# Settling three quarters of an FFN's output with factor and residual ahead of their last product

## The chip, the cores and the metric

The kernel runs on one core of a Trainium2 chip. The metric is device time in microseconds (us). The engines of the core run side by side, each through its own list of instructions in order: PE (matrix products), DVE (VectorE, elementwise), ACT (ScalarE, elementwise and functions), POOL (hardly used here), and SP, whose queue issues nearly all DMA transfers. PE writes to eight PSUM banks of 128x512 values; DVE and ACT read them.

## The reference, cut to what matters

One layer on 1024 tokens of width 1024, in float32: an FFN, a mixing sub-layer, a second FFN, a final norm. Each FFN adds half of its output to what came in:

```python
def rmsnorm(x, g):
    y = xf * lax.rsqrt(jnp.mean(xf * xf, axis=-1, keepdims=True) + NORM_EPS)
    return y * g

def swiglu_ffn(x, w_in, w_out):
    gate, up = jnp.split(x @ w_in, 2, axis=-1)
    return (jax.nn.silu(gate) * up) @ w_out
...
h = h + 0.5 * swiglu_ffn(rmsnorm(h, norm_ffn1), ffn1_w_in, ffn1_w_out)
u = rmsnorm(h, norm_mix)
proj = u @ w_in            # q, k, v, gates, pool: the mixing sub-layer follows
...
h = h + 0.5 * swiglu_ffn(rmsnorm(h, norm_ffn2), ffn2_w_in, ffn2_w_out)
return rmsnorm(h, norm_final)
```

The norm's root is one number per token. The kernel leaves it out of the products and multiplies the results by it afterwards; `rb` below is that row of numbers, halved (the 0.5), spread over the 128 partitions.

## The kernel before

Activations lie transposed: eight tiles `mt` of 128 channels by 1024 tokens. A *quarter* is one of these tiles on one half `j` of the tokens, 128x512. Products are made from pairs of float32r values, a high and a low part (`split`: ACT copies the high part, L158, DVE subtracts for the low part, L159), so each 128x128 by 128x512 product is three matmuls (`mm3`, L178 to L180).

All large products use Strassen's scheme in Winograd's form: seven block products in place of eight, whose sums make the four blocks of the result. The change is in `ffn_out`, the second half of an FFN. It is called twice: "b" after the first FFN, followed by the projections of the mixing sub-layer, and "d" after the second, followed by the end of the kernel (`last` is set there). Names in profile rows begin with that letter: `bacc` is a quarter or tile of b's result, `bp2w` the weight of step p2 in b, `bp2m` its moving operand, `bres` a residual, `brb` the factor row, `bL` the weight halves `L12` and `L22`, `br`, `bq`, `bT` and `bR` loaded activations.

`ffn_out` runs its block products in this order, each as FH = 11 steps over `k`, and each step on four banks `i`, that is twelve matmuls: p1 and p6 interleaved, p2 and p7 interleaved, p5, p3, and in b p4. In d p4 is made the other way round, tokens on the partitions: four tiles of 128 tokens, two in the steps `near`, two in `far`, which end the kernel. Banks "a" hold p1, then p1+p2; then p5, then p5+p3. Banks "b" hold p6, then p6+p7, then (in b) p4 too. After the last `k` of a product, `after1` to `after7` read each bank as soon as it is done:

- after p1: a copy of the bank to `p1s` (ACT). After p6: quarter (i, 1) = bank + `p1s` (`onto`).
- after p2: quarter (i, 0) = bank x `rb`, and `done`: plus the residual.
- after p7: quarter (i+4, 1) = bank + `p1s`. In b `p1s` is copied by ACT to quarter (i+4, 0); in d that quarter is bank + `p1s` and then `done`.
- after p5: quarter (i+4, 1) += bank, `done`. After p3: quarter (i, 1) += bank, `done`. After p4 (b): quarter (i+4, 0) += bank, `done`.

`done` puts a function `end` into a list of background work: scale the quarter by `rb` (L933; left out after p2), add the residual `old` (L941), hand the quarter to the next stage (`mix.quarter` in b: store it, square it on ACT, L264, and sum the squares, L265). With these four tiles finished, `end1` puts the next norm's operands into the list: R11 after p2, R22 after p5, T2, T1, T3 after p3, R21 and T4 after p4 (`n2R`, `n2T`), and at the end the norm's sums and root (`n2sum`, `n2v`, `n20b`, `n21b`). `t0` and `t1` are the first two groups of projections: `t0wL`, `t0wS` are weights, `t0a`, `t0b`, `t0e` banks, `t0v` a copy of a bank.

What sets the order: each step is a pair of functions. `Flow.run` calls the first (`prep`: loads, splits) four steps ahead of the second (`body`: the matmuls), and after each body takes two pieces of background work. A planner then orders the instructions on each engine; those within `soon()` have a high priority. Buffers come from small pools: `raw` has four tiles of 128x1024 (weight halves and residuals), `tl` four, `c2` eight of 128x512, `wt` five weights. A load is issued on SP's queue, in order, when the buffer that it fills is free. `residual(mts, j, tile, two)` loads the residuals of four quarters into two tiles of the pool named (or four of `c2`); it is called at k = FH - 3 of p2, p5, p3 and p4 (b) or p7 (d).

Of the kernel before, what the change touches and what calls it, by code (L numbers as in the profile page):

```python
# [15 lines left out]
ADD, SUB, MUL = ALU.add, ALU.subtract, ALU.mult  # L16
# [8 lines left out]
FH = FT // 2  # L25
# [65 lines left out]
def block_kernel(ctx: ExitStack, tc, x, x_tok, vecs, f1_in, f1_out, w_in, w_v, pool_w, w_ret, w_pool, w_o,  # L91
# [3 lines left out]
    tt = nc.vector.tensor_tensor  # L95
    stt = nc.vector.scalar_tensor_tensor
    act = nc.scalar.activation
    copy = nc.scalar.copy
    soon = tc.high_priority
    flow = Flow()  # L100
# [16 lines left out]
    def raw(name):  # L117
        return sb.tile([P, S], F32, tag="raw", bufs=N_RAW, name=name)

    def tl(name):  # L120
        return sb.tile([P, S], F32, tag="tl", bufs=N_TL, name=name)
# [4 lines left out]
    def c2(name):  # L126
        return sb.tile([P, H], F32, tag="c2", bufs=N_C2, name=name)
# [4 lines left out]
    def sum_bank(name):  # L132

        return ps.tile([P, H], F32, tag="sum", bufs=N_SUM, name=name)

    def load(dst, src):
        nc.sync.dma_start(dst, src)
# [8 lines left out]
    def half(t, j):  # L146
        return t[:, j * H : (j + 1) * H]
# [49 lines left out]
    for n in range(N_SUM):  # L197
        b = sum_bank(f"set{n}")
# [614 lines left out]
    def ffn_out(nx, ops, ready, w, res, name, sink, end, last=None):  # L813
# [4 lines left out]
        t, acc, old, p1s = {}, {}, {}, {}  # L818
# [4 lines left out]
            t["rb"] = sb.tile([P, S], F32, tag="mv", bufs=N_MV, name=f"{name}rb")  # L823
            act(t["rb"], nx.rms(), AF.Copy, scale=0.5)

        def residual(mts, j, tile, two=2):
            for n in range(0, 4, two):
                r = tile(f"{name}res{mts[n]}{j}")
                for z, mt in enumerate(mts[n : n + two]):
                    load(half(r, z), res[mt][:, j * H : (j + 1) * H])  # L830
                    old[mt, j] = half(r, z)

        TOP, LOW = range(4), range(4, 8)
# [6 lines left out]
        def both(key, k, src):  # L840

            if k % 2 == 0:
                t[key] = (tl if key[0] != "L" else raw)(f"{name}{key}{k}")
                n = min(2, FH - k)
                for z in range(n):
                    load(half(t[key], z), src(k + z))
            return half(t[key], k % 2)
# [21 lines left out]
            return s2, half(t["r"], 1)  # L869

        def p2(k):
            if k == FH - 3:
                residual(TOP, 0, raw)
            r = tl(f"{name}q{k}")
            load(half(r, 0), T[k][:, :H])
            load(half(r, 1), B[k][:, H:])
            t["r"] = r
            L12, s2 = both("L12", k, lambda z: w[z, :, 3 * H :]), half(S2[k // 2], k % 2)

            tt(s2, L12, s2, SUB)  # L880
            return L12, half(r, 0)

        def p7(k):
            if last and k == FH - 3:
                residual(LOW, 0, c2, 1)
            return half(S3[k // 2], k % 2), half(t["r"], 1)

        def p5(k):
            if k == FH - 3:
                residual(LOW, 1, raw)  # L890
            return half(S1[k // 2], k % 2), both("T1", k, lambda z: B[z][:, :H])

        def p3(k):
            if k == FH - 3:
                residual(TOP, 1, raw)
            return half(S2[k // 2], k % 2), both("R22", k, lambda z: T[z][:, H:])

        def p4(k):
            if not last and k == FH - 3:
                residual(LOW, 0, tl)  # L900
            return both("L22", k, lambda z: w[z, :, 2 * H : 3 * H]), both("T4", k, lambda z: T4[z])

        bk = {}
# [20 lines left out]
        def quarter(mt, j):  # L924
            return half(acc[mt], j)

        def onto(mt, j, where, i, before=None):
            q = quarter(mt, j)
            with soon():
                tt(q, bk[where, i], q if before is None else before, ADD)  # L930

        def scale(q, src, j):
            tt(q, src, half(t["rb"], j), MUL)  # L933

        def done(mt, j, to=sink, scaled=False):
            q = quarter(mt, j)

            def end():
                if not scaled:
                    scale(q, q, j)  # L940
                tt(q, q, old.pop((mt, j)), ADD)  # L941
                if to:
                    to(mt, slice(j * H, (j + 1) * H), acc[mt])

            flow.add(end)
# [4 lines left out]
                copy(p1s[i], bk["a", i])  # L950

        def after6(i):
            onto(i, 1, "b", i, p1s[i])

        def after2(i):
            with soon():
                scale(quarter(i, 0), bk["a", i], 0)
            done(i, 0, scaled=True)
            if i == 3:
                end(2)  # L960

        def after7(i):
            onto(i + 4, 1, "b", i, p1s[i])
            if last:

                onto(i + 4, 0, "b", i, p1s[i])
                done(i + 4, 0, None)
                if i == 3:
                    flow.add(*last.turned(acc))
            else:  # L970
                copy(quarter(i + 4, 0), p1s[i])

        def after5(i):
            onto(i + 4, 1, "a", i)
            done(i + 4, 1)
            if i == 3:
                end(5)

        def after3(i):
            onto(i, 1, "a", i)  # L980
            done(i, 1)
            if i == 3:
                end(3)

        def after4(i):
            onto(i + 4, 0, "b", i)
            done(i + 4, 0)
            if i == 3:
                end(4)

        for k in range(FH):
            yield step("p1", p1, k, "a", True, after1)
            yield step("p6", p6, k, "b", True, after6)
        for k in range(FH):
            yield step("p2", p2, k, "a", False, after2)
            yield step("p7", p7, k, "b", False, after7)
        for k in range(FH):
            yield step("p5", p5, k, "a", True, after5)
        for k in range(FH):
            yield step("p3", p3, k, "a", False, after3)  # L1000
        if not last:
            for k in range(FH):
                yield step("p4", p4, k, "b", False, after4)
            return
# [6 lines left out]
        def near(k):  # L1011
            def prep():
                l, r = p4(k)
                scale(r, r, 0)
                L[k], X[k] = operand(l, f"{name}p4w{k}"), mv(f"{name}p4m{k}")
                split(X[k][:, 0], X[k][:, 1], r)

            def body():
                if k == 1:

                    last.seed(2, bk["a", 0])
                    last.seed(3, bk["a", 1])
                for n in range(2):
                    turned(n, k)
                    if k == FH - 1:
                        last.finish(n)

            return prep, body
# [692 lines left out]
    class Last(Norm):  # L1721
# [76 lines left out]
        def end(self, part):  # L1798
            if part != 3:
                return  # L1800
            tokens = slice(H, S)
            at = {}

            def stats():
                r = inverse_root(token_sums(self.ssq, range(tokens.start // P, tokens.stop // P), "fin0"), D, "fin0")
                at["b"] = spread(r, "fin0")

            def scale(mt):
                t = self.tiles[mt][:, tokens]
                stt(t, t, vec[:, V_FINAL + mt : V_FINAL + mt + 1], at["b"], MUL, MUL)  # L1810
                load(out[mt, :, tokens], t)

            flow.add(stats, *(lambda mt=mt: scale(mt) for mt in range(KT)))
# [97 lines left out]
```

## Time and profile before

| what | value |
| --- | --- |
| time, median of 3 runs | 2169.99 us (2167.82 to 2172.97) |
| the profiled execution | 2169.06 us |
| its span, first to last instruction | 2167.2 us |
| mean granted TensorE clock | 0.996 |
| PE matmul, busy | 2145.4 us, 99% |
| DVE, busy | 1837.3 us, 85% |
| ACT, busy | 1091.1 us, 50% |
| DMA traffic | 320.91 MB, mean 148 GB/s |
| b: first p1 matmul to first p5 matmul | 423.5 to 543.2 us |

Rows of a profile are read so: in a table by stretch, the stretch in us, its length, then busy time (and count) of PE, PEld (weight loads, which overlap PE), DVE, ACT and POOL, the granted TensorE clock, the share of the DMA engines, and GB/s. In a timeline: start, duration, engine, line, operation, output<-inputs by the program's names, sizes, how many were merged into the row, and in brackets how long the engine had been idle and what ended the wait. DVE and ACT instructions overlap a little at their ends, so the distance of starts is what one costs. Matmuls too: each row has 0.39 us, while one starts every 0.23.

### The profile page before, as it was taken

How to read it: one execution, taken by the hardware profiler on the slowest of the kernel's cores; microseconds unless marked ns; L12 is line 12 of the kernel's file. 1: busy time of each engine (PE TensorE's matmuls, PEld its weight loads, DVE VectorE, ACT ScalarE, POOL GpSimd, SP SyncE). 2: the span in 40 equal slices, each digit the busy share in tenths (PEclk: the TensorE clock that was granted, in tenths of full speed). 3: DMA queues.
4: the chain of work that ended last, by engine and by line, in shares of the span. 5: the costliest groups of instructions: out<-in, count | busy, mean ns of one | idle time of the engine just before them, and what ended most of it. 6: DMA issues, size and time to landing. Idle time of an engine off the chain costs nothing.

```text
span 2167.2 us, 29645 instructions
## 1 busy us (share of the span) xinstructions
PE 2145.4 (99%) x10668; PEld 1815.0 (84%) x10668; DVE 1837.3 (85%) x3223; ACT 1091.1 (50%) x2053; POOL 0.2 (0%) x4
## 2 busy tenths in 40 slices
PE   9999999999989999999999999999999999999998
PEld 7888888888877888888888998887888888888887
DVE  8788888995897798899867877899988888889597
ACT  8544444553645444444435754446644544445454
POOL 0000000000000000000000000000000000000000
PEclk9999999999998999999999999999999999999999
DMA  7232423584532333233485567624223232358543
GB/s 260 87 114 82 136 75 128 182 287 137 184 128 102 117 113 121 88 127 108 160 276 181 166 206 255 246 91 159 74 85 135 74 127 93 127 176 287 184 122 126
DMA packets 120131, 320.91 MB, mean 148 GB/s; under 512 B 13232, under 2 KB 17456, under 8 KB 119984
## 3 DMA queue, kind: packets, MB, share of 16 engines
q1 hardware_dynamic: 119408, 317.98, 43.6%
q8 instruction: 83, 1.36, 0.3%
q10 hardware_dynamic: 576, 1.05, 0.1%
q14 instruction: 64, 0.52, 0.1%
HBM read 228.27 MB, written 90.70 MB: 147 GB/s over the span
## 4 chain that ended last, share of the span: by engine, by line
PE 91%; DVE 6%; ACT 1%; DMA 1%; issue 1%; SPq 0%; ACTq 0%; DVEq 0%
PE c_b L178 2%; PE c_b L180 2%; PE c_b L179 2%; PE a_b L178 2%; PE a_b L180 2%; PE a_b L179 2%; PE c_e L178 2%; PE c_e L179 2%; PE c_e L180 2%; PE a_e L178 2%; PE a_e L179 2%; PE a_e L180 2%; PE c_a L179 1%; PE a_a L178 1%; PE c_a L178 1%; PE c_a L180 1%
## 5 line engine op out<-in xcount | busy, mean ns | idle before, releaser
L179 PE MATMUL c_b<-n3T,c_wS 128*128 128x512 f32 x176 | 68.5, 389 | 0.0
L180 PE MATMUL c_b<-n3T,c_wS 128*128 128x512 f32 x176 | 68.5, 389 | 0.0
L178 PE MATMUL c_b<-n3T,c_wS 128*128 128x512 f32 x176 | 68.2, 389 | 0.0
L179 PE MATMUL a_b<-n1T,a_wS 128*128 128x512 f32 x168 | 65.4, 389 | 0.0
L178 PE MATMUL a_b<-n1T,a_wS 128*128 128x512 f32 x168 | 65.4, 389 | 0.0
L180 PE MATMUL a_b<-n1T,a_wS 128*128 128x512 f32 x168 | 65.4, 389 | 0.0
L179 PE MATMUL a_a<-n1R,a_wL 128*128 128x512 f32 x120 | 46.7, 389 | 0.0
L178 PE MATMUL a_a<-n1R,a_wL 128*128 128x512 f32 x120 | 46.7, 389 | 0.0
L180 PE MATMUL a_a<-n1R,a_wL 128*128 128x512 f32 x120 | 46.7, 389 | 0.0
L179 PE MATMUL c_a<-n3R,c_wL 128*128 128x512 f32 x112 | 43.7, 390 | 0.0
L178 PE MATMUL c_a<-n3R,c_wL 128*128 128x512 f32 x112 | 43.6, 389 | 0.0
L180 PE MATMUL c_a<-n3R,c_wL 128*128 128x512 f32 x112 | 43.6, 389 | 0.0
L178 PEld LDWEIGHTS c_b<-n3T,c_wS 128*128 128x128 f32 x176 | 33.0, 188 | 6.9
L180 PEld LDWEIGHTS c_b<-n3T,c_wS 128*128 128x128 f32 x176 | 33.0, 188 | 6.9
L179 PEld LDWEIGHTS c_b<-n3T,c_wS 128*128 128x128 f32 x176 | 33.0, 188 | 6.8
L159 DVE TENSOR_TENSOR a_wS<-a_S,a_wS 128x512 fp32r<-128x512 f32 x45 | 30.6, 682 | 9.1 <-ACT a_wS L158 9.0
L180 PEld LDWEIGHTS a_b<-n1T,a_wS 128*128 128x128 f32 x168 | 31.5, 188 | 6.6
L179 PEld LDWEIGHTS a_b<-n1T,a_wS 128*128 128x128 f32 x168 | 31.5, 188 | 6.5
L178 PEld LDWEIGHTS a_b<-n1T,a_wS 128*128 128x128 f32 x168 | 31.5, 188 | 6.5
L159 DVE TENSOR_TENSOR c_wS<-c_S,c_wS 128x512 fp32r<-128x512 f32 x46 | 31.3, 681 | 3.6 <-ACT c_wS L158 3.6
L178 PE MATMUL c_e<-n3T,c_wS 128*128 128x512 f32 x88 | 34.4, 391 | 0.0
L178 PE MATMUL c_e<-n3T,c_wL 128*128 128x512 f32 x88 | 34.4, 391 | 0.0
(3061 smaller groups left out, 8045.2 us busy)
## 6 DMA issues: line engine op xcount, KB each, us to landing
c_ra<-in_f_in SPq DMA_DIRECT2D x22, 512.0 KB, 3.5
c_rb<-in_f_in SPq DMA_DIRECT2D x22, 512.0 KB, 4.1
a_ra<-in_f_in SPq DMA_DIRECT2D x21, 512.0 KB, 3.7
a_rb<-in_f_in SPq DMA_DIRECT2D x21, 512.0 KB, 4.3
t<-au SPq DMA_DIRECT2D x11, 512.0 KB, 4.2
b<-ag SPq DMA_DIRECT2D x11, 512.0 KB, 3.6
r<-au SPq DMA_DIRECT2D x11, 512.0 KB, 3.6
br<-r SPq DMA_DIRECT2D x11, 512.0 KB, 5.3
```

Source lines behind the costliest of these rows:

```text
L159: tt(lo, src, hi.bitcast(F32), SUB)
L178: mm(dst, w[0], m[0], start=start, stop=False, skip_group_check=True)
L179: mm(dst, w[0], m[1], start=False, stop=False, skip_group_check=True)
L180: mm(dst, w[1], m[0], start=False, stop=stop, skip_group_check=True)
```

## The change

Three of the four groups of quarters that wait for a second product are *settled* while that product runs: the sum so far is multiplied by `rb` and the residual is added (`settle`). When the last product's bank is ready, it is multiplied by `rb` on its way out of PSUM into a `c2` tile `d`, and `d` is added to the quarter (`done`). So by linearity (sum + bank) x rb + residual becomes (sum x rb + residual) + bank x rb.

- Quarters (i, 1) are settled from k = 4 of p2 on, quarters (i+4, 0) from k = 8 of p2 on, straight out of `p1s` (so that ACT's copies in b go), quarters (i+4, 1) from k = 5 of p5 on.
- Quarters (i, 0) are not settled; their residual is added together with `d` after p2.
- The residuals are loaded in p2 at k = 1, 5 and 9 and in p5 at k = 1, all into `raw` tiles.

```diff
-        def residual(mts, j, tile, two=2):
-            for n in range(0, 4, two):
-                r = tile(f"{name}res{mts[n]}{j}")
-                for z, mt in enumerate(mts[n : n + two]):
+        def residual(mts, j):
+            for n in (0, 2):
+                r = raw(f"{name}res{mts[n]}{j}")
+                for z, mt in enumerate(mts[n : n + 2]):
                     load(half(r, z), res[mt][:, j * H : (j + 1) * H])
                     old[mt, j] = half(r, z)
...
         def p2(k):
-            if k == FH - 3:
-                residual(TOP, 0, raw)
+            if k == 1:
+                residual(TOP, 1)
+            if k == 4:
+                flow.add(*(lambda i=i: settle(i, 1) for i in range(4)))
+            if k == 5:
+                residual(LOW, 0)
+            if k == 8:
+                flow.add(*(lambda i=i: settle(i + 4, 0, p1s[i]) for i in range(4)))
+            if k == 9:
+                residual(TOP, 0)
...
         def p7(k):
-            if last and k == FH - 3:
-                residual(LOW, 0, c2, 1)
...
         def p5(k):
-            if k == FH - 3:
-                residual(LOW, 1, raw)
+            if k == 1:
+                residual(LOW, 1)
+            if k == 5:
+                flow.add(*(lambda i=i: settle(i + 4, 1) for i in range(4)))
...
         def p3(k):
-            if k == FH - 3:
-                residual(TOP, 1, raw)
...
         def p4(k):
-            if not last and k == FH - 3:
-                residual(LOW, 0, tl)
...
-        def onto(mt, j, where, i, before=None):
-            q = quarter(mt, j)
+        def onto(mt, j, where, i):
             with soon():
-                tt(q, bk[where, i], q if before is None else before, ADD)
+                tt(quarter(mt, j), bk[where, i], p1s[i], ADD)
...
-        def done(mt, j, to=sink, scaled=False):
+        def settle(mt, j, src=None):
+
             q = quarter(mt, j)
+            scale(q, q if src is None else src, j)
+            tt(q, q, old.pop((mt, j)), ADD)
+
+        def done(mt, j, where, i, to=sink):
+            q, d = quarter(mt, j), c2(f"{name}d{mt}{j}")
+            with soon():
+                scale(d, bk[where, i], j)
 
             def end():
-                if not scaled:
-                    scale(q, q, j)
-                tt(q, q, old.pop((mt, j)), ADD)
+                tt(q, old.pop((mt, j), q), d, ADD)
...
         def after2(i):
-            with soon():
-                scale(quarter(i, 0), bk["a", i], 0)
-            done(i, 0, scaled=True)
+            done(i, 0, "a", i)
...
         def after7(i):
-            onto(i + 4, 1, "b", i, p1s[i])
+            onto(i + 4, 1, "b", i)
             if last:
-                onto(i + 4, 0, "b", i, p1s[i])
-                done(i + 4, 0, None)
+                done(i + 4, 0, "b", i, None)
                 if i == 3:
                     flow.add(*last.turned(acc))
-            else:
-                copy(quarter(i + 4, 0), p1s[i])
...
         def after5(i):
-            onto(i + 4, 1, "a", i)
-            done(i + 4, 1)
+            done(i + 4, 1, "a", i)
```

`after3` and `after4` change as `after5` does. Nothing else in the kernel changes; in the changed kernel the bank reads by `rb` and the scalings of a settling are on L936, `onto` on L933, the residual of a settling on L942, the last add on L950, and the line L880 has become L888.

More of the change, by code (lines that the diff above doesn't have):

```diff
@@ L952, in after6 @@
         def after6(i):
-            onto(i, 1, "b", i, p1s[i])
+            onto(i, 1, "b", i)
         def after2(i):
-            with soon():
-                scale(quarter(i, 0), bk["a", i], 0)
-            done(i, 0, scaled=True)
+            done(i, 0, "a", i)
             if i == 3:
@@ L979, in after3 @@
         def after3(i):
-            onto(i, 1, "a", i)
-            done(i, 1)
+            done(i, 1, "a", i)
             if i == 3:
@@ L985, in after4 @@
         def after4(i):
-            onto(i + 4, 0, "b", i)
-            done(i + 4, 0)
+            done(i + 4, 0, "b", i)
             if i == 3:
```

## The prediction

> **What bounds the kernel now.** I read the page first, then the busy time by stretches, then the two stretches in which PE is not full, instruction by instruction on PE, DVE and ACT.
>
> ```profile
> PE 2145.4 (99%) x10668; PEld 1815.0 (84%) x10668; DVE 1837.3 (85%) x3223; ACT 1091.1 (50%) x2053; POOL 0.2 (0%) x4
> PE 91%; DVE 6%; ACT 1%; DMA 1%; issue 1%; SPq 0%; ACTq 0%; DVEq 0%
> 600.00:700.00 100.00, 90.58 (x379) 72.93 (x378) 87.64 (x161) 54.55 (x98) 0.00 (x0) 0.93 0.31 103
> 2130.00:2140.00 10.00, 9.11 (x45) 7.43 (x44) 9.39 (x17) 4.13 (x6) 0.00 (x0) 1.00 0.01 2
> ```
>
> PE bounds the whole: 99% busy, 91% of the chain. The second half of an FFN, `ffn_out`, runs from 423 to 633 us ("b") and again at the end ("d"). In it PE is full but for 0.89 us in the last row (DVE 9.39 of 10). Between 600 and 700, where b hands over to the projections, PE loses 9.42 us and part of its clock (0.93). So two places can give time back, and a stall anywhere else in b or d costs. PE at the handover:
>
> ```profile
> 633.37 0.39 PE L178 MATMUL t0a<-n2R,t0wL 128*128 128x512 f32 x1
> 633.60 0.39 PE L179 MATMUL t0a<-n2R,t0wL 128*128 128x512 f32 x1
> 636.94 0.50 PE L180 MATMUL t0a<-n2R,t0wL 128*128 128x512 f32 x1 [2.50 <-DVE t0wL L159]
> 650.38 0.80 PE L178 MATMUL t0b<-n2T,t0wS 128*128 128x512 f32 x1 [3.18 <-ACT t0v L479]
> 654.39 0.63 PE L178 MATMUL t0b<-n2T,t0wS 128*128 128x512 f32 x1
> 654.82 0.63 PE L179 MATMUL t0b<-n2T,t0wS 128*128 128x512 f32 x1
> 658.57 1.84 PE L228 MATMUL n2sum<-cst,n2ssq 128*128 128x1 f32 x16
> 668.19 0.78 PE L246 MATMUL n20b<-n20dg,ones_r 128*128 128x512 f32 x2 [2.17 <-ACT n20dg L245]
> 670.53 1.22 PE L246 MATMUL n21b<-n21dg,ones_r 128*128 128x512 f32 x2 [1.57 <-ACT n21dg L245]
> ```
>
> Four waits: 2.50 for a weight's low part, 3.18 for the copy `t0v`, 2.17 and 1.57 for the norm's factor. Starts lie 0.23 us apart at full clock (633.37, 633.60) and 0.43 after the second wait: 12 matmuls of half clock, 12 x 0.20 = 2.4 us more. DVE and ACT behind them:
>
> ```profile
> 601.79 2.48 DVE L930 TENSOR_TENSOR bacc<-bp5a,bacc 128x512 f32<-128x512 f32 x4
> 604.19 1.28 DVE L933 TENSOR_TENSOR bacc<-bacc,brb 128x512 f32<-128x512 f32 x2
> 605.39 1.29 DVE L941 TENSOR_TENSOR bacc<-bacc,bres 128x512 f32<-128x512 f32 x2
> 632.61 2.47 DVE L930 TENSOR_TENSOR bacc<-bp6b,bacc 128x512 f32<-128x512 f32 x4
> 636.21 0.68 DVE L159 TENSOR_TENSOR t0wL<-t0ra,t0wL 128x512 fp32r<-128x512 f32 x1
> 648.51 0.68 DVE L941 TENSOR_TENSOR bacc<-bacc,bres 128x512 f32<-128x512 f32 x1
> 661.03 0.15 DVE L214 TENSOR_SCALAR n2v<-n2sum 128x8 f32<-128x8 f32 x1
> 663.42 0.16 DVE L221 SCALAR_TENSOR_TENSOR n2r<-n2t,n2r 128x8 f32<-128x8 f32 x1
> 649.23 0.63 ACT L264 ACTIVATE n2q<-bacc 128x512 f32<-128x512 f32 x1 [1.16 <-DVE bacc L941]
> 666.63 0.19 ACT L158 CAST n20r<-n2r 128x4 fp32r<-128x4 f32 x1
> ```
>
> DVE works through one list without a rest. Both kernels can be built without running them, which gives the order of instructions on each engine (called the list here) and no times. In the list of before, 56 instructions stand from the first bank read of p3's end (601.79) to `t0wL` (636.21): 34.42/56 = 0.615 each, and 0.60 for a plain one, reading a bank or not (four from 601.79 to 604.19, two from there to 605.39). The last residual add (648.51) frees the fourth square on ACT (649.23), and only behind that comes `t0v`. The handover is bound by DVE's list.
>
> **The change, part by part.** Removed: at p5's, p3's and p4's ends a quarter took twelve DVE instructions (four bank reads, four scalings, four adds); now eight (four scaled bank reads into `d`, four adds). Where p2 ends the count stays eight. Also gone: b's four ACT copies at p7's end. Added: three settlings of eight DVE instructions in each of b and d, two in p2/p7 and one in p5. Per `ffn_out` DVE goes from 52 to 64 here, for both +24 x 0.60 = 14.4 us. What matters is the place.
>
> *b's handover.* From p3's end on the list loses the eight scalings, and small weight steps change places with the bank reads of p4's end, which the built order puts later.
> - `t0wL` is the 47th of the list, not the 57th: 601.79 + 46 x 0.615 = 630.1. PE wants it after 633.8, so the 2.50 goes, with 3 us to spare. p4's own operands, first needed by PE at 603, come no later than before.
> - The bank reads now come at 601.79 + 56 x 0.615 = 636.2 to 638.6. PE reaches `t0b` in those banks at 633.37 + 24 x 0.227 = 638.8, and the copies into them fit between on ACT. Cost nothing; if DVE is 2 us late there, PE waits that long.
> - The last add is the 68th, not the 77th: 648.51 - 9 x 0.60 = 643.1. From its start to PE's restart took 650.38 - 648.51 = 1.87, so `t0v` is ready at 645.0. PE is through the 48 matmuls ahead of it at 633.37 + 48 x 0.227 = 644.3. A wait of 0.7 stays of 3.18, and with so short a gap I take the half clock to go: 24 matmuls at 0.227 = 5.4, `n2sum` at 650.4 in place of 658.57, 8.2 earlier.
> - Late next is the root of the norm. `n2v` is the 89th, not the 97th: 661.03 - 8 x 0.60 = 656.2; root ready 2.55 later (661.03 to 663.58) at 658.8. The cast `n20r` (666.63) follows a cast that waits for PE, now at 658.4; so it runs at 658.9, 7.7 earlier. From there all keeps its distances. **b gives 7.7.** Bounds: 2.5, if only the first wait goes, and 10.1, if a second half clock goes too.
>
> *d's end.* The chain there:
>
> ```profile
> 2097.29 2.47 DVE L930 TENSOR_TENSOR dacc<-dp5a,dacc 128x512 f32<-128x512 f32 x4
> 2098.18 0.40 PE L178 MATMUL dp5a<-dp3m,dp3w 128*128 128x512 f32 x1
> 2138.94 1.02 PE L228 MATMUL fin0sum<-cst,n4ssq 128*128 128x1 f32 x8 [0.89 <-DVE n4ssq L265]
> ```
>
> The sum of squares comes four scalings (2.4) sooner, but the built order also puts `fin0sum` 11 matmuls (2.5) sooner: the 0.89 stays. At p5's end a bank must be read before p3 reuses it; 0.3 us were to spare (2097.29 + 0.60 against 2098.18), and the list ahead has one instruction fewer or more by how ACT and the loads fall. Bounds: 0.9 gained to 1.0 lost; taken 0, the count being level.
>
> *p2/p7: new work and moved loads.* Sixteen more DVE instructions, 9.6 us:
>
> ```profile
> 490.00:540.00 50.00, 50.00 (x222) 41.43 (x221) 24.94 (x40) 19.46 (x34) 0.00 (x0) 1.00 0.44 138
> 483.37 0.39 PE L178 MATMUL bp1a<-bp2m,bp2w 128*128 128x512 f32 x1
> 527.75 0.69 DVE L159 TENSOR_TENSOR bp2w<-bL,bp2w 128x512 fp32r<-128x512 f32 x1 [2.03 <-ACT bp2w L158]
> bL<-in_f_out SPq DMA_DIRECT2D x3, 256.0 KB, 3.8
> DMA to landing us min/median/max: 3.3/5.1/6.3
> ```
>
> DVE has 25 of 50 us free, so the instructions are covered. The loads are the risk. The residual tiles now sit in two of the four `raw` buffers, so an `L12` pair can be asked for only when the last split of the pair before is done; on SP's queue it stands behind residual loads that wait for a settling, and the operand loads behind it wait with it. DVE's list stops at the subtraction (L880, now L888) until the pair lands, 3.8 us by the group of these loads. I followed three pairs through the built lists: DVE stands up to 2 us at each, and the lead of 483.37 + 10 x 5.44 - 528.4 = 9.4 us that a `p2` weight has over PE (5.44 is (543.2 - 483.37)/11, a step of p2 and one of p7) falls to about 5.6. Cost nothing; without that cover, whatever a landing is longer than 3.8 + 5.6/3 = 5.7 us, three times a stage. The residual loads are the same bytes as before, only sooner. POOL's queue and ACT's have no part in it.
>
> *p5:* eight more instructions where DVE is full:
>
> ```profile
> 540.00:560.00 20.00, 20.00 (x90) 16.54 (x90) 19.91 (x33) 15.95 (x29) 0.00 (x0) 1.00 0.53 167
> 556.48 1.29 DVE L159 TENSOR_TENSOR bp5m<-bT,bp5m 128x512 fp32r<-128x512 f32 x2
> L178 PE MATMUL bp5a<-bp5m,bp5w x44: 389/389/390, 543.2 to 572.5; 128*128 128x512 f32 x44
> ```
>
> The operand of k = 8 (556.48) stands eight places later, ready at 556.48 + 4.8 + 0.7 = 562.0; PE wants it at 543.2 + 8 x 2.72 = 565.0 (the last row; 2.72 is half of 5.44). Three us are left, the tightest place; cost nothing. What is pushed out is p3's operands, wanted from 573 on. The second residual tile of this settling waits on SP for p2's last adds, with the early p4 weights behind it; p3's operand loads queue there too, and land some 5 us ahead of their use.
>
> *Sum:* 7.7 + 0. The profiled run took 2169.06 (span 2167.2 and 1.9 around it); less 7.7 is 2161.4. The median shown, 2169.99, is 0.9 higher, so I forecast 2162.3.
>
> **The clock, row and rule.** The 2.50 us wait halved nothing, the 3.18 wait did. By the Trainium skill, "TensorE: Matmul & The Clock Gate", part 1, the gate falls after an idle window of about 3.4 us and the windows run free of the kernel. By that rule 0.7 us of waiting cannot halve the clock, which agrees with the sum above; but the half clock after `n21b` may come or not by where the windows fall.
>
> **Rivals.**
> - *The second half clock goes too.* For it: the whole handover moves by 7.7 us against whatever times the gate; against: its two waits of 2.17 and 1.57 stay, and the first may grow by 0.5. Those 12 matmuls save another 2.4: 2159.9. This is what the rule of free windows allows.
> - *The wait moves to `t0v`.* ACT's list still holds it behind four squares, each after an add (1.16 us waits), and the adds now also need `d` tiles, eight `c2` buffers that the squares share. If they come no sooner, only the 2.50 goes: 2167.5, within 0.2%. Against: nine instructions fewer on an unbroken list.
> - *Slower: late `L12` pairs.* Place and price above: at a landing of 8 us each pair is 4.2 late, 12.6 in three, less the 5.6: PE stalls 7.0 and then runs 12 matmuls at half clock (2.4), in b and in d: 18.8 - 7.7 = 11.1 slower, 2181.1. It begins to cost at 5.7 and turns the sign at about 7.0. For it: single landings reach 6.3. Against: the group's 3.8.
> - *It doesn't do what it says:* DVE's list at the handover is held by weight loads, not its length: 2170.0. Against: no DMA is named in its waits there.
>
> **How the numbers follow.** Forecast 0.59, second clock 0.12, wait moved 0.13, late pairs 0.12, no effect 0.04. 0.2%, 4.3 us, is about what a measurement of this kernel can tell from no change. Faster by more: 0.59 + 0.12 = 0.71; within: 0.13 + 0.04 = 0.17; slower: 0.12. The range runs from the second clock with half a spread of the three runs off (2.5) to the moved wait with as much on: 2157.5 to 2170.0; late pairs and a little of no effect stay out.
>
> **What would show it.** Right: `t0wL` before PE's p4 ends and no PE wait there; under 1 us at `t0v`; `n2sum` 8 us sooner; PE full through both p2/p7 and p5. Wrong: a PE wait for `p2w`, `p7w` or `p5m`, or for a bank at p3's start; DVE waiting for `L12` longer than 2 us; half clock still after `t0v`.

## The result, and the profile after

The changed kernel took 2160.45 us (median of six runs, 2159.65 to 2160.76), the kernel before 2169.78 us (six runs, 2165.6 to 2172.97): a ratio of 0.9959, 95% interval 0.9946 to 0.9971. The profiled execution took 2160.41 us; its span is 2158.6, 8.6 us less than before, and its mean granted clock 0.998 in place of 0.996. The forecast of 2162.3 was 1.85 us too high.

The page and the stretches of the changed kernel that answer to those of before:

```profile
PE 2143.2 (99%) x10668; PEld 1813.2 (84%) x10668; DVE 1849.4 (86%) x3247; ACT 1089.6 (50%) x2049; POOL 0.2 (0%) x4
PE 92%; DVE 5%; ACT 1%; issue 1%; DMA 1%; SPq 0%; ACTq 0%; DVEq 0%
```

```profile
490.00:540.00 50.00, 50.00 (x222) 41.40 (x221) 35.27 (x59) 19.45 (x34) 0.00 (x0) 1.00 0.55 179
540.00:560.00 20.00, 20.00 (x90) 16.57 (x89) 20.00 (x34) 13.37 (x24) 0.00 (x0) 1.00 0.49 154
600.00:700.00 100.00, 95.18 (x413) 77.43 (x412) 89.89 (x164) 56.73 (x102) 0.00 (x0) 0.97 0.28 98
```

DVE has 12 us more to do in all, 10.3 of them from 490 to 540 (24.94 to 35.27), and PE is still full there. From 600 to 700 PE's busy time rises from 90.58 to 95.18 and the clock from 0.93 to 0.97. So most of the time came from b's handover, as forecast. The timeline of PE in it:

```profile
645.52 0.50 PE L178 MATMUL t0b<-n2T,t0wS 128*128 128x512 f32 x1 [0.94 <-ACT t0v L479]
...
651.12 1.84 PE L228 MATMUL n2sum<-cst,n2ssq 128*128 128x1 f32 x16
...
660.86 1.02 PE L246 MATMUL n20b<-n20dg,ones_r 128*128 128x512 f32 x2 [2.29 <-ACT n20dg L245]
663.45 1.22 PE L246 MATMUL n21b<-n21dg,ones_r 128*128 128x512 f32 x2 [1.57 <-ACT n21dg L245]
664.47 0.63 PE L178 MATMUL t0e<-n2T,t0wS 128*128 128x512 f32 x1
664.90 0.63 PE L179 MATMUL t0e<-n2T,t0wS 128*128 128x512 f32 x1
```

The 2.50 for `t0wL` is gone, the wait for `t0v` is 0.94 in place of 3.18, and no half clock follows it. The two waits for the norm's factor stay (2.29 and 1.57), and so does a stretch of half clock, which begins between the two (at 661.91): `t0e`'s matmuls start 0.43 us apart. DVE and ACT behind PE:

```profile
602.22 2.48 DVE L936 TENSOR_TENSOR bd<-bp5a,brb 128x512 f32<-128x512 f32 x4
...
630.84 0.68 DVE L159 TENSOR_TENSOR t0wL<-t0ra,t0wL 128x512 fp32r<-128x512 f32 x1
...
636.98 2.47 DVE L936 TENSOR_TENSOR bd<-bp6b,brb 128x512 f32<-128x512 f32 x4
...
643.59 0.68 DVE L950 TENSOR_TENSOR bacc<-bacc,bd 128x512 f32<-128x512 f32 x1
...
656.72 0.15 DVE L214 TENSOR_SCALAR n2v<-n2sum 128x8 f32<-128x8 f32 x1
...
644.90 0.57 ACT L479 COPY t0v<-t0b 128x512 f32<-128x512 f32 x1
...
659.30 0.19 ACT L158 CAST n20r<-n2r 128x4 fp32r<-128x4 f32 x1
```

Each of them is where the list put it, 0.4 to 0.8 us late: 630.8 for 630.1, 637.0 for 636.2, 643.6 for 643.1, 656.7 for 656.2, 659.3 for 658.9. Most of that is there from the first row on: the list starts at 602.22, not at 601.79. The last fence says why (three rows of p2's weights, then p5's and p3's):

```profile
477.95 0.69 DVE L888 TENSOR_TENSOR bs<-bL,bs 128x512 f32<-128x512 f32 x1 [2.02 <-DMA bL<-in_f_out]
478.56 0.69 DVE L159 TENSOR_TENSOR bp2w<-bL,bp2w 128x512 fp32r<-128x512 f32 x1
...
508.55 0.68 DVE L159 TENSOR_TENSOR bp2w<-bL,bp2w 128x512 fp32r<-128x512 f32 x1
...
561.19 0.69 DVE L159 TENSOR_TENSOR bp5m<-bT,bp5m 128x512 fp32r<-128x512 f32 x1
...
572.63 2.48 DVE L936 TENSOR_TENSOR bd<-bp5a,brb 128x512 f32<-128x512 f32 x4
573.46 0.47 PE L178 MATMUL bp5a<-bp3m,bp3w 128*128 128x512 f32 x1
```

p5 starts at 543.28 and has 132 matmuls of 0.227, so p3 could start at 573.2. It starts at 573.46, when the first bank read (572.63) is through: 0.3 us lost that the forecast had not counted. The next matmul is held up by 0.1 us too, so that p4 starts at 603.48, where it started at 603.05 before.

The projections start no later for it (`t0a` at 633.40, before at 633.37). From p4's first matmul to `t0a` it took 30.32 us before and takes 29.92 now: before, PE waited in p4 for low parts of an operand, of which this is the longest (a weight load of the kernel before), and now it doesn't.

```profile
623.23 0.19 PEld L179 LDWEIGHTS bp6b<-bp4m,bp4w 128*128 128x128 f32 x1 [0.41 <-DVE bp4m L159]
```

### The profile page after: what moved, and what is told of

It is laid out like the page before. It is cut to its first block, busy times and chain, and to the rows that moved or that the text cites. A ratio compares the mean times of both kernels' runs of the same rounds, so it can differ in the third digit from the quotient of the medians.

```text
span 2158.6 us, 29681 instructions
## 1 busy us (share of the span) xinstructions
PE 2143.2 (99%) x10668; PEld 1813.2 (84%) x10668; DVE 1849.4 (86%) x3247; ACT 1089.6 (50%) x2049; POOL 0.2 (0%) x4
## 4 chain that ended last, share of the span: by engine, by line
PE 92%; DVE 5%; ACT 1%; issue 1%; DMA 1%; SPq 0%; ACTq 0%; DVEq 0%
PE c_b L178 2%; PE c_b L180 2%; PE c_b L179 2%; PE a_b L178 2%; PE a_b L179 2%; PE a_b L180 2%; PE c_e L178 2%; PE a_e L179 2%; PE c_e L179 2%; PE a_e L178 2%; PE c_e L180 2%; PE a_e L180 2%; PE a_a L179 1%; PE a_a L180 1%; PE a_a L178 1%; PE c_a L179 1%
```

## Experiments

All times beside an experiment are medians, and the ratios are to the kernel before, run on the same chip: 2168.86 us beside b alone, d alone, the kernel without scalings and the one without p5's settling; 2167.59 beside the two on the room in p5 and p2, the matmuls of eight columns and the early root; 2169.40 beside the other four. Where a stage is compared between traces, it is by the distance between the first matmuls of two stages, since starts shift from one execution to the next (b's p5 starts between 542.6 and 544.3 us).

### Which of the two calls gives the time

The first kernel has the changed `ffn_out` for b and the old one (`ffn_old`) for d, the second the other way round:

```diff
-   ffn_out(ffn2, ops2, ..., f2_out, h2, "d", fin.quarter, fin.end, fin)
+   ffn_old(ffn2, ops2, ..., f2_out, h2, "d", fin.quarter, fin.end, fin)
```

> The changed code in b alone, d as before. Theory (the gain is b's handover; in the two traces everything behind b lies 7.1 to 7.7 us earlier, and d adds 0.7 to 0.9 with the 0.89 us wait of fin0sum): 2161.3 us, from 2160.8 to 2162.0, with n2sum near 651 us and the wait of 0.89 at fin0sum back. Rival (the prediction's own term: d gives 0): the same as the whole change, 2160.5.

> The changed code in d alone, b as before. Theory (d gives 0.7 to 0.9): 2169.0 us, no PE wait at fin0sum, and all four waits of b's handover as in the kernel before. Rival (the prediction's term: d gives 0, so what the trace shows of 0.9 is a shift from b): 2169.8 with a wait at fin0sum.

b alone: 2162.88 us (2160.68 to 2163.48; 2161.3 was expected), ratio 0.9969 (0.9957 to 0.9980). d alone: 2168.35 us, ratio 0.9994 (0.9986 to 1.0003), which is no difference that the times can tell; all four waits of the handover are there as before. The sizes come from the traces. b alone has the handover of the whole change to a tenth: from `t0a` to `t0e` 31.08 us, against 31.07 in the changed kernel and 38.18 before. The end of d (timelines of b alone, then of d alone):

```profile
2132.89 1.02 PE L228 MATMUL fin0sum<-cst,n4ssq 128*128 128x1 f32 x8 [0.66 <-DVE n4ssq L265]
```

```profile
2135.73 1.02 PE L228 MATMUL fin0sum<-cst,n4ssq 128*128 128x1 f32 x8
```

With the old code in d PE waits 0.66 to 0.89 us at `fin0sum`, with the new one not at all here and in the changed kernel, and up to 0.17 in kernels below with the same d. From d's p4 to the last instruction it takes 39.06 us before, 38.89 with b alone, 38.42 with d alone, 38.36 with both, and 37.96 to 38.39 in the kernels below whose end of d is that of the changed kernel. So d's end gives 0.5 to 1.1 us, where the forecast had 0, and b nearly all the rest.

### Do the settlings cost anything?

This is the kernel before without the scalings in `done`: the factor is left out for three groups of quarters, and nothing is added in their place.

```diff
             def end():
-                if not scaled:
-                    scale(q, q, j)
                 tt(q, q, old.pop((mt, j)), ADD)
```

> The kernel before without the scalings in done: three of the four groups of quarters are not multiplied by the factor row, which is left out of the computation. DVE's list to the handover is then exactly as short as in the changed kernel, but nothing is added in p2, p7 and p5, and the residuals are loaded where they were. Theory (only the length of the list at the handover counts, the settlings and the moved loads cost nothing): within 1 us of the changed kernel, 2160.5, waits at t0v of 0.9 and at n20b of 2.3. Rival (the settlings or the late L12 pairs eat part of the gain): faster than the changed kernel by what they eat, 2159 or less. Rival (the list is not what binds): 2167 to 2170.

2161.64 us, ratio 0.9967 (0.9954 to 0.9980): not faster than the changed kernel. PE has no wait for `t0v`, and `n2sum` comes 16.55 us after `t0a` (17.72 in the changed kernel, 25.20 before). `n2v`, which DVE's list places, comes 83.06 us after p3's first matmul, against 83.26. So the list behind p3 is as short as the changed kernel's, and the settlings take nothing from the handover that shows (0.2 us at `n2v`). `n20b` comes 0.8 us later than in the changed kernel by the same count: ahead of it lies one stretch of half clock more, and ACT's cast ahead of the factor's waits 0.96 us for PE's `t1a`, which it doesn't in the changed kernel. These are two stretches of this kernel, the columns as in the tables before:

```profile
649.20:652.60 3.40, 3.22 (x23) 2.62 (x21) 3.40 (x7) 2.68 (x5) 0.00 (x0) 1.00 0.02 5
652.68:656.09 3.41, 3.41 (x8) 2.44 (x9) 3.41 (x7) 1.71 (x3) 0.00 (x0) 0.50 0.01 2
```

PE counts as busy for 3.22 of the 3.40 us ahead of it, and yet the clock falls for 3.41. Sixteen of those 23 matmuls are `n2sum`'s, of one column each (1.84 us). That is taken up below.

### Which quarter's settling gives the time

Three kernels leave one group of quarters unsettled. The first:

```diff
         def p5(k):
-            if k == 1:
+            if k == FH - 3:
                 residual(LOW, 1)
-            if k == 5:
-                flow.add(*(lambda i=i: settle(i + 4, 1) for i in range(4)))
...
         def after5(i):
-            done(i + 4, 1, "a", i)
+            q = quarter(i + 4, 1)
+            with soon():
+                tt(q, bk["a", i], q, ADD)
+            def finish():
+                settle(i + 4, 1)
+                sink(i + 4, slice(H, S), acc[i + 4])
+            flow.add(finish)
```

The second does the same to quarters (i, 1) at p3's end, both in b and in d; the third to quarters (i+4, 0) at p4's end, in b only (there ACT's copies come back too).

> The changed kernel with quarters (i+4, 1) not settled in p5: bank read, scaling and residual at p5's end as before, residual loaded late in p5. Theory (the handover is set by the part of DVE's list behind p3's end; the twelve instructions behind p5 are worked off before, since DVE is busy only 4.6 of the 10 us from 590 to 600): the same as the changed kernel within 0.5 us, 2160.5. Rival (every shortened quarter counts equally, a third of the gain goes with it): 2163.5.

> The changed kernel with quarters (i, 1) not settled in p2: bank read, scaling and residual at p3's end as before. Behind p3's end DVE's list is then four instructions, 2.4 us, longer. Theory (idle time of DVE takes a part: it is busy 8.39 of the 10 us from 600 to 610, so 1.6 us are free): n20b 0.8 us later, 2161.3, from 2160.5 to 2162.9. Rival (each of the four counts in full at the handover): n20b 2.4 us later, 2162.9.

> The changed kernel with quarters (i+4, 0) not settled in b: at p4's end bank read, scaling and residual as before, ACT's copies back (d as changed). DVE has no rest from 620 us on. Theory (each instruction of the list behind p4 costs its 0.60 at the handover): t0wL in time, wait at t0v 0.94 + 2.4 = 3.3 us, n2v and n20b 2.4 us later: 2162.9, and up to 2165 if the longer wait halves the clock again. Rival (the first wait and the clock are what the change gained, not the list's length behind p4): n20b as in the changed kernel, 2160.5.

| left out | time, us | ratio (95%) | `n20b` after p5's start, us |
| --- | --- | --- | --- |
| nothing (run again, below) | 2160.91 | 0.9960 (0.9947 to 0.9972) | 117.58 and 118.25 |
| (i+4, 1), p5 | 2160.91 | 0.9960 (0.9946 to 0.9973) | 117.23 |
| (i, 1), p3 | 2163.19 | 0.9970 (0.9961 to 0.9980) | 120.58 |
| (i+4, 0), p4 | 2164.33 | 0.9982 (0.9973 to 0.9991) | 121.68 |

(The first of the three was run on another chip than the rest of the table, beside 2168.86 us.) The settling in p5 gives nothing, as expected: between p5's end and p3's DVE has idle time, from 590 to 600 us still 3.2 of 10 without this settling. It even costs a little. From p5's first matmul to p3's takes 29.92 us before and in the kernel without this settling, and 30.18, 30.82 and 30.35 in the changed kernel, in its second trace and in b alone: the bank reads at p5's end come late.

The settling at p3's end was expected to be worth 0.8 and is worth 2.3 to 3.0 by the table, 2.2 counted from p3's first matmul, which leaves p5's end out (`n20b` after 89.63 us, against 87.40 and 87.43). The table by stretch was misread: DVE's idle time between 600 and 610 lies ahead of the first bank read, not behind it, and from there the list has no rest (changed kernel):

```profile
601.61 0.69 DVE L159 TENSOR_TENSOR bp4w<-bL,bp4w 128x512 fp32r<-128x512 f32 x1 [2.03 <-ACT bp4w L158]
602.22 2.48 DVE L936 TENSOR_TENSOR bd<-bp5a,brb 128x512 f32<-128x512 f32 x4
604.62 1.28 DVE L950 TENSOR_TENSOR bacc<-bacc,bd 128x512 f32<-128x512 f32 x2
605.82 0.68 DVE L159 TENSOR_TENSOR bp4w<-bL,bp4w 128x512 fp32r<-128x512 f32 x1
```

All four instructions count (4 x 0.60 = 2.4), and PE meets a wait that was hidden so far (timeline of the kernel without the settling at p3's end):

```profile
642.86 0.50 PE L178 MATMUL t0b<-n2T,t0wS 128*128 128x512 f32 x1 [1.65 <-ACT t0b L474]
...
649.54 0.50 PE L178 MATMUL t0b<-n2T,t0wS 128*128 128x512 f32 x1 [0.90 <-ACT t0v L479]
```

This is the case that the forecast named for the bank reads behind p4: 2.4 us more on DVE's list ahead of them, and PE waits 1.65 for a copy into `t0b`. Without the settling at p4's end the wait for `t0v` is back (PE, then ACT):

```profile
648.00 0.54 PE L178 MATMUL t0b<-n2T,t0wS 128*128 128x512 f32 x1 [3.09 <-ACT t0v L479]
...
662.74 0.62 ACT L158 CAST t0wL<-t0rb 128x512 fp32r<-128x512 f32 x1 [1.40 <-PE t1a L180]
```

3.3 was expected. Counted from p3's first matmul `n2v` is 2.3 us later, which is the four instructions, and `n20b` 3.7 (91.12). The other 1.4 come by way of PE, which is late after the wait and the 3.41 us of half clock that follow it: ACT's cast ahead of the factor's now waits 1.40 us for `t1a`, where in the changed kernel it waited for nothing. In times the two settlings are worth 2.3 and 3.4 us of the 8.5 on this chip (2169.40 - 2160.91); they don't add up to it, and in neither kernel does PE wait for `t0wL`, whose 2.5 us are gained already.

### How much room is left in p5 and p2

The first kernel compares each quarter (i+4, 1) with itself twice ahead of its settling: eight DVE instructions more in p5, which change no value.

```diff
             if k == 5:
-                flow.add(*(lambda i=i: settle(i + 4, 1) for i in range(4)))
+                def twice(i):
+                    q = quarter(i + 4, 1)
+                    for _ in range(2):
+                        tt(q, q, q, ALU.max)
+                    settle(i + 4, 1)
+                flow.add(*(lambda i=i: twice(i) for i in range(4)))
```

> The changed kernel with eight more DVE instructions in p5 (each quarter (i+4, 1) is compared with itself twice ahead of its settling, which changes no value). In the list the operand of k = 8 then stands 8 x 0.60 = 4.8 us later, 561.9 to 566.7 us, and PE wants it at 565.2. Theory (3.3 us is the margin in p5 and nothing behind gives it back): one PE wait of about 1.5 us for bp5m in b, none in d, where p5 has 11 us; 2162.0, from 2161.0 to 2163.5. Rival (p5 has more slack than the list tells): 2160.5 with no wait. Rival (every DVE instruction there costs its own 0.60): 2165 in b, 2170 with d.

```profile
565.53 0.69 DVE L159 TENSOR_TENSOR bp5m<-bT,bp5m 128x512 fp32r<-128x512 f32 x1
...
564.58 1.07 PE L178 MATMUL bp5a<-bp5m,bp5w 128*128 128x512 f32 x4
566.27 0.50 PE L179 MATMUL bp5a<-bp5m,bp5w 128*128 128x512 f32 x1 [0.62 <-DVE bp5m L159]
```

The low part of k = 8 is ready at 566.2, 0.5 before the 566.7 expected, because p5 itself starts 0.46 earlier in this execution: the margin of 3.3 us is right. PE waits 0.62, not 1.5, since the planner put the four matmuls that need only the high part ahead (x4 in the second row). p5 takes 30.84 us to p3, 0.7 more than in the first trace of the changed kernel and no more than in its second (30.82). In the time (2159.55 us, ratio 0.9963, 0.9949 to 0.9978) this isn't to be seen.

The other kernel loads half of p5's residuals at k = 1 of p2 already, into a third one of the four `raw` buffers:

```diff
             if k == 1:
                 residual(TOP, 1)
+                raw_low = raw(f"{name}reslow")
+                for z in range(2):
+                    load(half(raw_low, z), res[4 + z][:, H:])
+                    old[4 + z, 1] = half(raw_low, z)
```

> The changed kernel with half of p5's residuals (one raw tile, two quarters) loaded already at k = 1 of p2, so that one of the four raw buffers fewer is left for the L12 pairs all through p2. Theory (the lead of 6.8 us that p2's weights have is worn down by each pair's landing): DVE waits for L12 longer than now (3 to 4 us at a pair, where it was 2.0 at most), the lead sinks below 4 us but is not used up: 2160.5 to 2161. Rival (the pairs become the bound, as in the prediction's slower case): PE waits for bp2w, 2163 to 2170.

2160.00 us, ratio 0.9965 (0.9953 to 0.9977). The time was right and the reason wrong: DVE waits 1.1 us for `bL` in all of b (5.0 in the changed kernel), and the weight of k = 6 is ready 7.8 us ahead of PE, more than the 6.8 of the changed kernel. The planner orders the instructions anew for this kernel, and in its list the subtractions that need a pair stand where the pair is nearly always there. So this run doesn't show how late a pair may be; the slower rival stays without a test of its own. It shows the other tight place again, at p3's start:

```profile
573.18 2.48 DVE L940 TENSOR_TENSOR bd<-bp5a,brb 128x512 f32<-128x512 f32 x4
...
574.01 0.47 PE L178 MATMUL bp5a<-bp3m,bp3w 128*128 128x512 f32 x1 [1.35 <-DVE bd L940]
```

### The clock, and a faster version

Two kernels give PE idle matmuls in the wait for the norm's factor; their results are overwritten by the first real matmul into the bank. The first has nine of eight columns ahead of `n20b` and four of 512 columns ahead of `n21b`; the second has one small one and then only matmuls of 512 columns (this is its diff):

```diff
     def spread(r, name):
...
+        if name == "n20":
+            mm(b[:, :8], ones, fill["t"], start=True, stop=True, ...)
+        for _ in range({"n20": 5, "n21": 4}.get(name, 0)):
+            mm(b, ones_r, fill["m"], start=True, stop=True, ...)
```

(`fill["t"]` is `n2t`, so that they can't run earlier; `fill["m"]` is an operand that is there.)

> The changed kernel with idle matmuls ahead of n20b (nine of 128x8, 18 passes, about 2 us, as soon as n2t is there) and ahead of n21b (four of 128x512, 0.9 us); what they write is overwritten by the first real matmul. By the built order four matmuls of t0e move ahead of n21b. Theory (the half clock after n21b comes from PE standing still, 2.3 and 1.6 us within 5): no half clock behind t0e, 2.4 us less, and 0.4 to 0.9 from the four moved matmuls: 2157.5, from 2157.0 to 2158.5. Rival (idle matmuls of eight columns don't count as work, or the clock falls for another reason): half clock stays, 2160.

> The changed kernel with idle matmuls of full width (128x512) in the wait for the norm's factor: one small one that waits for n2t, five ahead of n20b and four ahead of n21b; the planner then puts t0e's first matmuls between them. Theory (the clock follows how full PE is, and the eight columns of the first try counted as idle): no half clock at all in the handover, and with t0e's matmuls in place of waiting the work behind them 4 us sooner: 2156.5, from 2155.5 to 2158. Rival (the clock falls from the 0.94 us at t0v and the short matmuls of n2sum, whatever follows): half clock of 3.4 us or more stays, 2158.5 to 2160.

Eight columns: 2160.88 us, ratio 0.9964 (0.9952 to 0.9977). The matmuls fill the wait, and the clock falls all the same, for 3.41 us (6.83 in the first trace of the changed kernel, 3.41 in the second). From `t0a` to the third group of matmuls (`t0b` from `n2R`) it takes 36.56 us, 0.9 less than in that second trace (37.46), which the time doesn't show:

```profile
659.11 2.17 PE L242 MATMUL n20b<-n2t,cst 128*128 128x8 f32 x18
```

```profile
658.10:661.50 3.40, 3.29 (x24) 2.70 (x22) 3.33 (x12) 3.15 (x8) 0.00 (x0) 1.00 0.72 239
661.57:664.98 3.41, 3.41 (x8) 2.48 (x8) 1.26 (x7) 2.07 (x6) 0.00 (x0) 0.50 0.65 216
```

Full width: 2156.85 us (2155.87 to 2156.99), ratio 0.9942 (0.9929 to 0.9956), the lowest median of all kernels here, and the clock is full through the handover:

```profile
640.00:680.00 40.00, 38.96 (x180) 31.81 (x179) 36.45 (x75) 26.03 (x48) 0.00 (x0) 1.00 0.32 118
```

From `t0a` to the third group it takes 34.02 us, against 38.56 and 37.46 in the two traces of the changed kernel: 4.5 and 3.4 us, where 4 was expected. Of the 4.5 us 2.4 are twelve matmuls at half clock (12 x 0.20); the rest goes with `t0e`'s matmuls, which the planner now puts into the wait.

Another version gives the steps of the norm's root high priority:

```diff
-                self.r_tok = inverse_root(t, D, self.name)
+                with soon():
+                    self.r_tok = inverse_root(t, D, self.name)
```

> The changed kernel with the steps of every norm's root at high priority, so that in DVE's list n2v stands 9 places earlier and the rest of the root close behind it. Theory (what is left of the handover is bound by the root's place in DVE's list): n2v at about 653.2 us in place of 656.7, the factor 3 us sooner; PE's wait at n20b under 1.5 us in place of 2.3, with n20b moved up by the planner into t1a: 2 to 3 us less, 2158, with 2155.5 if the half clock goes too. Rival (the wait only moves, since n20b now stands ahead of work that PE could do): 2160.5 or slower.

2157.83 us (2155.98 to 2159.37), ratio 0.9955 (0.9942 to 0.9969), where 2158 was expected. From `t0a` to the third group it takes 35.38 us, and no half clock falls into it in this trace. `n2v` is early, and the wait at `n20b` is gone, but two others are there, since DVE now stands still for `n2sum` ahead of the weights' low parts:

```profile
652.42 0.17 DVE L214 TENSOR_SCALAR n2v<-n2sum 128x8 f32<-128x8 f32 x1 [1.73 <-PE n2sum L228]
...
654.44 0.50 PE L180 MATMUL t0a<-n2R,t0wL 128*128 128x512 f32 x1 [1.48 <-DVE t0wL L159]
...
658.50 0.50 PE L180 MATMUL t1a<-n2R,t1wL 128*128 128x512 f32 x1 [1.04 <-DVE t1wL L159]
```

The changed kernel once more:

> The changed kernel once more, beside the three others. Theory (before loses up to four stretches of half clock of 3.41 us in the handover, the changed kernel one or two, so that its times lie closer together): 2159.5 to 2161, granted clock 0.998 or 0.999 in all, where before has 0.994 to 0.998 and 2165 to 2173. Rival (the narrow spread of the first six runs was chance): runs of the changed kernel up to 2164 with a clock of 0.996.

2160.91 us (2159.02 to 2161.44), clock 0.998 or 0.999 in each of five runs. Before, on the same chip, has 19 runs from 2165.39 (clock 0.998) to 2173.56 (0.995). A thousandth of clock goes with 2 to 3 us there, so much of the spread of the kernel before goes with how long the clock is down, and a part of the gain is that the changed kernel gives it less occasion: at the same clock of 0.998 the two are some 4 us apart (2165.39, a single run, against 2160.91 and 2161.44).

## Why the prediction was right, point by point

- *b's handover, 7.7.* From `t0a` to the third group of projections PE took 45.97 us before and 38.56 after: 7.4. The chain is the one that was worked out: `t0wL` in time, 0.94 at `t0v` (0.7 forecast), then the root of the norm as the limit. The handover has twice 6.83 us of half clock before and once after. `n2sum` is 7.45 sooner (8.2 forecast), `n20b` 7.33 (7.7). Without the settlings at p3's or p4's end 2.3 and 3.4 us of the time go.
- *p5's end, 0.* This is the term that was mis-sized. The forecast named 0.3 us to spare for the bank reads and took nothing; p3 starts 0.3 us late in the profiled run, 0.1 to 1.0 late in most other kernels that keep the settling and 1.5 with a residual held, and everything on DVE's list behind it with it. The kernels without the settling in p5 have none of it. In the sum it was made good by luck, by the 0.4 us that PE no longer loses in p4 (without the settling at p3's end it loses them again, 30.32). The forecast had p4's operands no later than before, and nothing for their coming sooner.
- *p5's operands.* Ready at 561.9 (561.19 and 0.69) as forecast (562.0), 3.3 us ahead of the first matmul that needs it; eight instructions more use it up.
- *p2 and p7, 0.* PE is full. One wait of DVE for an `L12` pair is 2.02 us, the others shorter, and the weight of k = 6, ready at 509.23, is wanted at 483.44 + 6 x 5.44 = 516.08: the lead there is 6.8, where it was forecast to fall to 5.6. The least is another, that of the first weight, behind the 2.02 us: ready at 479.25, wanted at 483.44, a lead of 4.2 (4.7 in the second trace, 6.8 before). So the margin was smaller than forecast, which had followed the lead of the last weight. Over the whole kernel DVE's 24 new instructions are 12.1 us of busy time, where 14.4 was worked out.
- *d, 0.* Its end gives 0.7 in the profiled run: the 0.89 at `fin0sum` was to stay because its matmuls move ahead in PE's order, and it went. The sum of squares was early enough for both. The forecast's own bounds (0.9 gained to 1.0 lost) held it.
- *The clock.* The half clock behind `t0v` went, and the one at `n21b` stayed, as taken; but how long it lasts is a matter of the single execution (6.83 and 3.41 us in the two traces). The rival of the second half clock came true only where the waits for the factor were filled or broken up.
- *The sum.* 7.4 in the handover, 0.4 in d (222.57 to 222.17 us from its first matmul to the end), and 0.8 in the 1265 us between, where the two traces of the changed kernel themselves differ by 1.0, so it isn't put down to the change: 8.6 in all, of which the forecast has 7.7. The forecast for the profiled time was 2161.4, measured 2160.41. The other 0.9 us of the miss is the step from there to the median: it added to the changed kernel the 0.9 by which the median of before lay above its profiled run. That distance lies within the spread of the kernel before, and the changed kernel's spread is smaller (1.1 us in its first six runs, 7.4 before).
- *The other rivals.* The wait did not move to `t0v`, DVE's list was what bound, and no `L12` pair was late enough to stop PE; how late one may be was not tried. The forecast's 7.0 us, at which late pairs would turn the sign, leaves out the half clock that its own price counts: 2 x (3 x (7.0 - 3.8) - 5.6) = 8.0, but with 2 x 2.4 of half clock the 7.7 would be lost at 6.1 already.

## What to carry to other kernels

Where an elementwise engine works through one unbroken list into a handover, look for the engine's last idle gap, and move work across it: here an instruction taken out of the list behind the last place where DVE had to wait was worth its full 0.60 us, and one put in ahead of that place cost next to nothing. The places just ahead of a bank's reuse are the exception, as p5's end shows. Short rests of PE can cost twice, once as the wait and once as the clock, and idle matmuls of full width in them paid for themselves here. The distance between a median and a profiled run belongs to the kernel that has it; don't carry it over to a changed one.

## What the runs showed of the hardware

The clock changes in steps of 3.41 us, and how many columns PE works through in a fixed stretch of that length goes with the clock of the next. In twelve of the fourteen traces the granted clock falls at the handover, always for 3.41 or 6.83 us, and the full stretches between are whole multiples too (13.65 is four, 1488.21 is 436), so the edges don't move within an execution. Laid out in steps of 3.41 from the first fall, with 0.227 us for each matmul of 512 columns and less in proportion for fewer (twice that at half clock), counted from its start, the stretches from 600 to 690 us divide so:

| what follows the stretch | stretches | PE filled with columns, share |
| --- | --- | --- |
| full clock, then half | 16 | 0.07 to 0.38 |
| full clock, stays full | 262 | 0.44 and more |
| half clock, stays half | 10 | 0.32 to 0.78 |
| half clock, then full | 16 | 0.86 and more |

At half clock a column takes twice the time, so in plain columns the two halves of the table are one rule: after each stretch with 2992 columns or fewer (26 of them) the next is at half clock, after each with 3292 or more (278) at full, whichever clock it had itself. A full stretch has 7700. The table was drawn from the traces after they had run; ahead of its run only the kernel with idle matmuls of full width put the idea to the test. How sharp the limit is depends on where in its record a matmul is counted: by the records' middles the first two rows close up to 0.41 and 0.43, and by their ends they touch at 0.43.

That explains what a list of waits can't: before, the 2.50 us at `t0wL` halves nothing because the edge of a stretch divides it (shares of 0.64 and 0.54), and the 3.18 us at `t0v` does, with one stretch at 0.38. `n2sum`'s matmuls of one column and the idle ones of eight count as nearly nothing, though the profile shows PE busy through them. The Trainium skill, "TensorE: Matmul & The Clock Gate", part 1, has free-running windows of about 3.4 us, which agrees with the 3.41 here; but it lets the clock fall after an idle window, and here a window filled to 0.38 was enough.
